# Keeping mLSTM's q and k of a block on the chip, and a shorter ring for the sampled keys while the inputs are projected

## The chip, the cores and the metric

The kernel is one program on one core of a Trainium2 chip. The core has five engines with a queue each: TensorE (PE in the profile; its weight loads are listed apart as PEld), VectorE (DVE), ScalarE (ACT), GpSimd (POOL) and SyncE (SP). Each takes its instructions in the order of the program, and an instruction whose data isn't ready holds up all that stand behind it on that engine. Transfers between DRAM and the on-chip memory (SBUF) are issued here mostly by SP; those that gather rows by an index are issued by POOL. All of them share 16 DMA engines. Matmul results land in PSUM, eight banks of 128 x 512 float32.

The metric is the device time of one execution in microseconds (us), the median of several runs.

## The reference, cut to what matters

One layer of a decoder is computed for 2048 new tokens of one prompt and for 8 sampled sequences of 8 tokens each, which have 8192 earlier tokens in a paged cache.

```python
z = x @ w_in                                    # 1024 -> 3600 columns
fq, fk, fv, f_gate = ...                        # FoX: 8 heads of 64
qk_in, mv, i_gate, f_gate, o_gate = ...         # mLSTM: 4 heads of 128
qk = silu(conv4(qk_in))                         # causal, 4 taps, per channel
mq, mk = qk[..., :512], qk[..., 512:] * 128**-0.5
# FoX: attention with a decay, s += L_q - L_k, softmax, @ v
#   prompt: 2048 x 2048 causal; sampled: 8 x (8192 cached + 8 new)
# mLSTM, chunk by chunk:
Wqk = exp(Dm - m_t) * (q @ k.T)
num = Wqk @ v + (q @ C) * a                     # C: 128 x 128 per head
h   = num / max(|Wqk.sum() + (q @ n) * a|, exp(-m_t))
C   = g * C + (w_key * k).T @ v                 # carried to the next chunk
mix = concat([fox_h, norm(h) * w * o_gate]) @ w_o
x1  = LN(alpha * x + mix)
y   = LN(alpha * x1 + relu(x1 @ w1)**2 @ w2)
```

All is float32. The large products are made of three matmuls with rounded high and low halves (`mm3`), whose halves ScalarE (`split_hi`) and VectorE (`split_lo`) make.

## The kernel before, in words

The program runs in four stages, one after the other.

**Stage A**, the input projection (`block_a`), goes over four blocks of 512 prompt tokens; the first also has the 64 sampled tokens. In a block the columns come in this order: mLSTM's v, mLSTM's q and k (eight groups `j` of 128 channels, each followed by its convolution `conv`), the output gate, FoX's q, k and v. For each piece of 256 columns or tokens, 24 matmuls go into one of four PSUM banks `pm`, and ScalarE or VectorE takes the bank away. In `conv` ScalarE copies the bank into `qi` (two buffers), VectorE multiplies and adds four times into `ac`, ScalarE takes the tanh into `th`, and VectorE makes `(th + 1) * ac`. `ac` and `th` share three buffers. The result is stored to the DRAM array `dqk` (line 468).

**Beside** stage A run two side streams, Python generators that give out a few instructions at each `yield`. `tick(us)`, called after each piece of the projection with the piece's nominal time, takes one step of a stream whenever the summed time passes a pace. The instructions of a step are placed behind the projection's last ones. A scheduler then orders each engine's queue.

- The first stream holds mLSTM (`PACE_M` 2.3): `gate_stream` makes the decay rows of a block, `m_block` goes over its four chunks of 128 tokens, and `m_sample` does the sampled tokens after the first block. A chunk loads its q and k from `dqk` into `qk`, one buffer (`m_load_qk`, line 592). `m_sample` goes over four heads, and each loads its states into `C0`, in the same buffer as `qk` (line 748), and stores them.
- The second is the sampled attention (`sample_attention`). A prologue computes the decays over the cache (in the first stream, ahead of `m_block(0)`). Then come 294 numbered steps (`PACE_A` 7.5). Step `n` gathers piece `n` of the keys (128 x 1024 float32, POOL, `k_gather`, line 1376), turns piece `n-2` in 32 x 32 squares on VectorE (`k_turn`, line 1382, two instructions a piece), and at every fourth step TensorE multiplies four pieces with the queries (`qk_step`, lines 1405 and 1412). The pieces live in `KB`, three pairs of two. Every eighth `qk_step` is followed at once by `softmax` (line 1424), and later steps weigh the values (`v_gather`, `pv_step`, line 1517).

The time of stage A's first block is added to the second stream's account although it has no stream yet, so that at the start of block two some nineteen steps are due at once.

**Stage B** is the prompt's FoX attention. It gives the sampled attention no step (`PACE_B` is infinite). It begins with keys that are loaded, doubled by POOL (`twice`, line 866), transposed by TensorE (line 885) and split. **Stage O** applies `w_o` and the first norm, **stage C** the MLP in four blocks. The sampled attention goes on beside both (`PACE_C` 5).

Of the kernel before, what the change touches and what calls it, by code (L numbers as in the profile page):

```python
# [20 lines left out]
PACE_A = 7.5  # L21
PACE_B = float('inf')
PACE_C = 5
PACE_M = 2.3
# [28 lines left out]
def body(ctx, tc, I, O, stages):  # L53
# [8 lines left out]
    dqk = drm.tile([8, 128, TOT], F32, name="dqk")  # L62
# [34 lines left out]

    acc = [0.0, None, PACE_A]
    macc = [0.0, []]
    last = {}  # L100

    vx = dict(more=None, live=[], next=0, of={})

    def take_back():

        vx["more"] = None
        while 1 in vx["live"] and acc[1] is not None:
            if beside(acc[1]) == 0:
                acc[1] = None
# [7 lines left out]

    def tick(us):

        macc[0] += us  # L120
        while macc[1] and macc[0] > PACE_M:
            macc[0] -= PACE_M
            if beside(macc[1][0]) == 0:
                macc[1].pop(0)
# [3 lines left out]
        while acc[1] is not None and acc[0] > acc[2]:  # L128
            acc[0] -= acc[2]
            if beside(acc[1]) == 0:  # L130
                acc[1] = None
# [272 lines left out]
    def block_a(bi):  # L404
# [31 lines left out]
        macc[1].insert(0, gate_stream(bi))  # L436

        for j in range(8):
# [20 lines left out]
            def conv(src, dst, n):  # L459
                ac = pa.tile([128, 512], F32, name="ac", tag="ac", bufs=3)[:, :n]  # L460
# [4 lines left out]
                th = pa.tile([128, 512], F32, name="th", tag="ac", bufs=3)[:, :n]  # L465
                A.activation(th, ac, AF.Tanh)
                V.scalar_tensor_tensor(th, th, 1.0, ac, op0=OP.add, op1=OP.mult)
                SY.dma_start(dst, th)

            conv(lambda q: qi[:, q:q + 512], dqk[j, :, t0:t0 + 512], 512)  # L470
            if pre:
                conv(lambda q: qs[:, :, q:q + 8], dqk[j, :, S:], 64)
# [32 lines left out]
        for j in range(4):  # L505
            if j % 2 == 0:
                wh, wl = wload([(j * 128, 256)])
                if pre:
                    qr = ps_.tile([32, 8, 8, 8], F32, name="qr", bufs=1)
            cs = slice((j % 2) * 128, (j % 2) * 128 + 128)  # L510
            st = pa.tile([128, 512], F32, name="qst", tag="ac", bufs=3)
            for i in range(2):
# [9 lines left out]
                A.activation(st[:, i * 256:i * 256 + 256], ps[:, w - 256:], AF.Copy, scale=0.125)  # L522
            SY.dma_start(dq[j, :, t0:t0 + 512], st)
            if pre and j % 2 == 1:
                SY.dma_start(dqb[0, :, :, j // 2 * 64:j // 2 * 64 + 64].rearrange("b p c -> p b c"), qr.rearrange("p b i t -> p b (i t)"))
        for i in range(2):
# [10 lines left out]
            natural(sink, (512 + i * 256, 256))  # L537
        for i in range(2):
# [9 lines left out]
    dqkv = dqk.rearrange("j p t -> p j t")  # L548
# [41 lines left out]
    def m_load_qk(c):  # L590
        qk = pm.tile([128, 8, 128], F32, name="qk", bufs=1)
        SY.dma_start(qk, dqkv[:, :, c * 128:c * 128 + 128])
        return qk

# [11 lines left out]
    def m_block(bi):  # L606
# [6 lines left out]
        qk = m_load_qk(bi * 4)  # L613
# [4 lines left out]
        for c in range(bi * 4, bi * 4 + 4):  # L618
            Cs = mst["C"]
            t0 = c * 128  # L620
            yield 1
# [27 lines left out]
            for p in range(2):  # L649
                yield 1  # L650
                if p == 1 and c % 4 < 3:
# [965 lines left out]
```

## Time and profile before

| | |
|---|---|
| median of 3 runs | 3457.11 us (3455.04 to 3475.27) |
| the profiled execution | 3461.98 us, of which 3460.3 us from first to last instruction |
| TensorE busy | 3291.5 us (95%) |
| VectorE, ScalarE, GpSimd busy | 2170.0, 1365.9, 876.3 us |
| granted TensorE clock, mean | 0.975 |
| moved by DMA | 663.16 MB |

Stage A ends about 1000 us after the start, stage B about 1420 us; the rest is O and C. A row of the stretches shows, for a window of time, each engine's busy time with the number of its instructions, the clock that TensorE was granted, and the DMA engines' busy share. A row of the waits says which engine's instruction stood idle, what it waited for, and then the total, the number and the longest of these waits in us. In a timeline, the bracket at the end of a row is the engine's idle time just before it and what ended it.

### The profile page before, as it was taken

The numbers are of one execution on the slowest core, as the hardware profiler recorded it, in microseconds if no ns is written. First come the engines' busy times: TensorE is split into PE (matmuls) and PEld (weight loads), VectorE is DVE, ScalarE is ACT, GpSimd is POOL, SyncE is SP. The second block draws the span as 40 slices with busy tenths as digits, with TensorE's granted clock in tenths as the row PEclk, the third lists the DMA queues.
The fourth block names the chain that finished last, engine by engine and source line by source line (L and its number), as shares of the span: only waits on it lengthen the run. The fifth ranks groups of instructions, "written<-read, shape, count | busy, mean of one in ns | idle before, by whom it ended". The sixth has DMA issues, their size and how long they took to land.

```text
span 3460.3 us, 59595 instructions
## 1 busy us (share of the span) xinstructions
PE 3291.5 (95%) x22428; PEld 2695.6 (78%) x22428; DVE 2170.0 (63%) x5282; ACT 1365.9 (39%) x2818; POOL 876.3 (25%) x962
## 2 busy tenths in 40 slices
PE   8899999898989999999799999999999999999998
PEld 8898888887976767677577777777776777888887
DVE  4948646655658877556566667766666545755455
ACT  3333233332448888622233233332333333443332
POOL 0023122232332222266423333423333110100000
PEclk9899899999999999999899999999999999999999
DMA  5577676776772232377776866868668554442221
GB/s 172 145 211 251 190 210 220 236 240 198 240 221 79 80 82 65 108 260 264 270 241 228 278 234 239 315 208 300 243 209 296 202 179 155 153 137 74 86 86 64
DMA packets 446040, 663.16 MB, mean 192 GB/s; under 512 B 84604, under 2 KB 333760, under 8 KB 444856
## 3 DMA queue, kind: packets, MB, share of 16 engines
q1 hardware_dynamic: 369064, 380.13, 36.3%
q0 software_dynamic: 74304, 270.57, 21.3%
q10 hardware_dynamic: 2384, 8.65, 0.7%
q8 instruction: 177, 2.90, 0.3%
q14 instruction: 111, 0.91, 0.1%
HBM read 598.01 MB, written 61.22 MB: 191 GB/s over the span
## 4 chain that ended last, share of the span: by engine, by line
PE 42%; DMA 4%; issue 2%; DVE 1%; POOL 1%; ACT 0%; SPq 0%; POOLq 0%; ACTq 0%; DVEq 0%
PE py L147 7%; PE py L148 6%; PE py L149 6%; PE ph L147 6%; PE ph L148 6%; PE ph L149 6%; PE sO L1517 2%; DMA wr<-w 2%; PE sQ L1405 1%; DMA kT<-cache_k,idxK 1%; DMA vt<-cache_v,idxV 1%; PE sT L1474 1%; DVE wl L142 0%; DMA y_prompt<-y 0%; POOL kT L1376 0%
## 5 line engine op out<-in xcount | busy, mean ns | idle before, releaser
L1206 DVE TENSOR_TENSOR y<-y,py 128x512 f32<-128x512 f32 (+1 forms) x476 | 320.5, 680 | 267.8 <-PE py L149 263.7
L147 PE MATMUL ph<-x1h,wh 128*128 128x512 f32 (+1 forms) x1280 | 454.3, 355 | 6.4 <-ACT wh L139 5.1
L1382 DVE STREAM_TRANSPOSE kT<-kT 128x512 f32<-128x512 f32 x512 | 330.0, 685 | 199.2 <-DMA kT<-cache_k,idxK 198.9
L149 PE MATMUL ph<-x1h,wl 128*128 128x512 f32 (+1 forms) x1280 | 452.4, 355 | 2.1 <-DVE wl L142 2.0
L148 PE MATMUL ph<-x1l,wh 128*128 128x512 f32 (+1 forms) x1280 | 453.6, 355 | 0.0
L139 ACT ACTIVATE wh<-wr 128x1024 fp32r<-128x1024 f32 x264 | 273.0, 1056 | 439.6 <-PE py L149 232.1
L1376 POOL DMA_INDIRECT kT<-cache_k,idxK x256 | 262.1, 1024 | 715.1 <-PE sQ L1405 645.8
L147 PE MATMUL py<-wh,hh 128*128 128x512 f32 (+1 forms) x1088 | 432.3, 399 | 8.2 <-DVE y L1206 7.7
L148 PE MATMUL py<-wl,hh 128*128 128x512 f32 (+1 forms) x1088 | 427.7, 393 | 0.9 <-DVE wl L142 0.9
L149 PE MATMUL py<-wh,hl 128*128 128x512 f32 (+1 forms) x1088 | 426.6, 393 | 0.0
L142 DVE TENSOR_TENSOR wl<-wr,wh 128x1024 fp32r<-128x1024 f32 x264 | 328.4, 1249 | 90.4 <-PE ph L149 33.0
L147 PE MATMUL pm<-whi,xh 128*128 128x256 f32 (+2 forms) x1088 | 323.9, 298 | 3.5 <-DVE xl L142 2.7
L148 PE MATMUL pm<-wlo,xh 128*128 128x256 f32 (+2 forms) x1088 | 314.8, 289 | 0.0
L149 PE MATMUL pm<-whi,xl 128*128 128x256 f32 (+2 forms) x1088 | 314.1, 289 | 0.0
L147 PEld LDWEIGHTS ph<-x1h,wh 128*128 128x128 f32 x1280 | 241.7, 189 | 46.4 <-ACT wh L139 5.7
L149 PEld LDWEIGHTS ph<-x1h,wl 128*128 128x128 f32 x1280 | 241.2, 189 | 38.5 <-DVE wl L142 4.0
L148 PEld LDWEIGHTS ph<-x1l,wh 128*128 128x128 f32 x1280 | 241.5, 189 | 35.4 <-issue 2.1
L147 PEld LDWEIGHTS py<-wh,hh 128*128 128x128 f32 (+1 forms) x1088 | 201.3, 185 | 64.3 <-DVE y L1206 12.1
L149 PEld LDWEIGHTS py<-wh,hl 128*128 128x128 f32 (+1 forms) x1088 | 201.3, 185 | 50.4 <-issue 3.3
L147 PE MATMUL pm<-xh,whi 128*128 128x256 f32 (+1 forms) x768 | 227.2, 296 | 8.9 <-ACT qi L456 8.9
L148 PEld LDWEIGHTS py<-wl,hh 128*128 128x128 f32 (+1 forms) x1088 | 201.5, 185 | 43.1 <-issue 2.9
L149 PE MATMUL pm<-xh,wlo 128*128 128x256 f32 (+1 forms) x768 | 225.0, 293 | 0.0
(364 smaller groups left out, 6823.5 us busy)
## 6 DMA issues: line engine op xcount, KB each, us to landing
wr<-w SPq DMA_DIRECT2D x256, 512.0 KB
wra<-w_in SPq DMA_DIRECT2D x112, 512.0 KB
xn<-x_prompt SPq DMA_DIRECT2D x32, 512.0 KB
Rb<-dR SPq DMA_DIRECT2D x128, 128.0 KB
dqk<-th SPq DMA_DIRECT2D x32, 256.0 KB
qk<-dqk SPq DMA_DIRECT2D x16, 512.0 KB
qn<-dq SPq DMA_DIRECT2D x128, 64.0 KB
wr<-w_o SPq DMA_DIRECT2D x16, 512.0 KB
```

The costliest lines, as they stand in the source:

```text
L139: last["ACT"] = A.activation(dst, src, AF.Copy, scale=scale)
L142: r = (eng or V).tensor_tensor(dst, src, hi.bitcast(F32), op=OP.subtract)
L147: T.matmul(ps, wh, xh, start=first, stop=False)
L148: T.matmul(ps, wh, xl, start=False, stop=False)
L149: last["PE"] = T.matmul(ps, wl, xh, start=False, stop=stop)
L1206: V.tensor_tensor(y, y, ps, op=OP.add)
L1376: G.indirect_dma_start(out=piece(n), out_offset=None, in_=ck, in_offset=IO(ap=idxK[:, b, j // 2, j % 2:j % 2 + 1], axis=0))
L1382: V.transpose(x, x)
L1405: r = T.matmul(pq[h4 * 32:h4 * 32 + 32, hg].rearrange("p (k f c) -> p k f c", k=2, f=4), z["qb"][:, hd], kv, start=(db == 0), stop=(db == ...
L1474: T.transpose(p[:, f], z["U"][u][:, hg, f].rearrange("p k t -> p (k t)"), ident)
L1517: after_ = T.matmul(po[r:r + 32], z["PT"][:, hg, 2 * f + g, pg].rearrange("p h q -> p (h q)"), vts[f][:, g, hg * 256:(hg + 1) * 256], star ...
```

## The change

q and k of a whole block stay in SBUF: `conv` writes its last product straight into `mst["qk"]`, four chunks of 8 x 128, one buffer for the block; the tanh goes into the space of `qi`, so that `ac` has its two buffers to itself. The stores to `dqk` and the loads of `m_load_qk` are gone, but for the 64 sampled tokens. Before the convolution of the next block begins, what is left of the `m_block` before it is placed.

The sampled attention becomes the second stream from the first block on, prologue included, at pace 5.6, and starts its steps once block one's sampled keys are made. In stage A its ring has two pairs, that is the four pieces of one `qk_step`; two pieces are gathered in each of the first two steps of a group of four, and two are turned in each of the last two. After 19 groups it stops (`yield 3`). Behind stage A a new ring of three pairs is made in a pool of its own, and six pieces are gathered into it at the start of stage B. `softmax` comes one step after the last `qk_step` instead of in the same one, and `softmax_new` two steps after that.

`m_sample` loads the states of a head one head ahead, in the two buffers of tag `vt` that later hold the values. FoX's q is stored in two halves of 256 tokens instead of one of 512.

```diff
-PACE_A = 7.5
+PACE_A = 5.6
-    dqk = drm.tile([8, 128, TOT], F32, name="dqk")
+    dqk = drm.tile([8, 128, NS], F32, name="dqk")
...
+        while mst.get("open"):
+            beside(macc[1][0]) or macc[1].pop(0)
+        mst["qk"] = pm.tile([128, 4, 8, 128], F32, name="qk", bufs=1)
         for j in range(8):
...
-            def conv(src, dst, n):
-                ac = pa.tile([128, 512], F32, name="ac", tag="ac", bufs=3)[:, :n]
+            def conv(src, th, out):
+                n = th.shape[1]
+                ac = pa.tile([128, 512], F32, name="ac", bufs=2)[:, :n]
...
-                th = pa.tile([128, 512], F32, name="th", tag="ac", bufs=3)[:, :n]
                 A.activation(th, ac, AF.Tanh)
-                V.scalar_tensor_tensor(th, th, 1.0, ac, op0=OP.add, op1=OP.mult)
-                SY.dma_start(dst, th)
-            conv(lambda q: qi[:, q:q + 512], dqk[j, :, t0:t0 + 512], 512)
+                V.scalar_tensor_tensor(out, v(th), 1.0, v(ac), op0=OP.add, op1=OP.mult)
+            conv(lambda q: qi[:, q:q + 512], qi[:, 0:512], mst["qk"][:, :, j])
...
-    def m_load_qk(c):
-        qk = pm.tile([128, 8, 128], F32, name="qk", bufs=1)
-        SY.dma_start(qk, dqkv[:, :, c * 128:c * 128 + 128])
-        return qk
...
+        def state(h):
+            c = ps_.tile([128, 8, 128], F32, name="C0", tag="vt", bufs=2)
+            SY.dma_start(c, I["state_C"][0, :, h].rearrange("b d e -> d b e"))
+            return c
...
+        C0s = [state(0), state(1)]
...
         for h in range(4):
-            C0 = pm.tile([128, 8, 129], F32, name="C0", tag="qk", bufs=1)
-            SY.dma_start(C0[:, :, 0:128], I["state_C"][0, :, h].rearrange("b d e -> d b e"))
-            G.tensor_copy(C0[:, :, 128], n0[:, :, h])
-            for _ in range(4):
-                yield 1
+            C0 = C0s[h]
+            yield 1
+            if 1 <= h < 3:
+                C0s.append(state(h + 1))
...
         if bi == 0 and gen:
-            macc[1].append(prologue(gen))
+            acc[0], acc[1] = 0.0, gen
...
+    kx["ring"] = pk_.tile([128, 3, 2, 1024], F32, name="kT", bufs=1)
+    acc[1] = acc[3]
+    if acc[1] is not None:
+        attend()
...
-    KB = ps_.tile([128, 3, 2, 1024], F32, name="kT", tag="kT", bufs=1)
+    kx["ring"] = pa.tile([128, 2, 2, 1024], F32, name="kT", tag="kT", bufs=1)
+    GA = 19
+    NA = 4 * GA
...
-        if 2 <= n < 258:
+        g, r = divmod(n - 2, 4)
+        if 0 <= g < GA and r >= 2:
+            k_turn(4 * g + 2 * r - 4)
+            k_turn(4 * g + 2 * r - 3)
+        if NA + 2 < n < 258:
+            if n == NA + 3:
+                k_turn(NA)
             k_turn(n - 2)
...
-            if g % 8 == 7:
-                softmax(g // 8)
+        b = at(n, 35, 32)
+        if b is not None and b < 8:
+            softmax(b)
...
-        if n < 256:
+        g, r = divmod(n - 2, 4)
+        if 0 <= g < GA and r < 2:
+            k_gather(4 * g + 2 * r)
+            k_gather(4 * g + 2 * r + 1)
+        if NA + 6 <= n < 256:
             k_gather(n)
...
     for n in range(294):
         yield 1
         step(n)
+        if n == NA + 2:
+            yield 3
+            for i in range(6):
+                k_gather(NA + i)
```

94 lines of the change are left out of this document (54 added, 40 removed).

## The prediction, made before the changed kernel ran

> **What bounds the kernel now.** I read the page's first two parts, then the stretches of the stages, then the waits. TensorE is busy nearly all the time, and its clock dips in the first 30% and at a few later places:
>
> ```profile
> PE 3291.5 (95%) x22428; PEld 2695.6 (78%) x22428; DVE 2170.0 (63%) x5282; ACT 1365.9 (39%) x2818; POOL 876.3 (25%) x962
> PEclk9899899999999999999899999999999999999999
> ```
>
> The stretches are stage A, B, and O with C:
>
> ```profile
> 0.00:1000.00 1000.00, 911.90 (x7686) 857.82 (x7686) 621.39 (x1727) 333.27 (x720) 228.82 (x272) 0.95 0.68 210
> 1000.00:1420.00 420.00, 408.92 (x2806) 288.10 (x2804) 334.46 (x1326) 346.67 (x974) 111.56 (x195) 0.98 0.32 88
> 1420.00:3460.00 2040.00, 1970.71 (x11940) 1549.65 (x11939) 1214.15 (x2229) 685.92 (x1125) 535.91 (x495) 0.99 0.60 204
> ```
>
> Stage A takes 29% of the span and has half of TensorE's idle time: 1000 - 911.9 = 88.1 us, against 11.1 in B and 69.3 in O and C. And its clock was 0.95: another 0.05 x 1000 = 50 us in which TensorE counts as busy and does nothing more. So A holds some 138 us that aren't work. What an idle TensorE costs beyond its own time is seen around two stalls (third last column: the granted clock):
>
> ```profile
> 842.70:845.70 3.00, 0.04 (x1) 0.00 (x0) 0.00 (x0) 1.27 (x2) 2.26 (x3) 1.00 0.93 322
> 845.70:859.40 13.70, 4.19 (x49) 4.20 (x50) 5.49 (x18) 0.41 (x1) 0.55 (x1) 0.50 0.53 196
> 187.90:190.40 2.50, 0.61 (x6) 0.62 (x6) 1.22 (x1) 1.42 (x3) 1.06 (x2) 1.00 1.00 281
> 190.40:193.80 3.40, 3.40 (x18) 3.40 (x18) 0.00 (x0) 1.53 (x5) 0.63 (x1) 0.50 0.98 269
> ```
>
> A long stall at 843 us is followed by 13.7 us at half clock, but an idle stretch of 2.5 - 0.61 = 1.9 us at 188 us by 3.4 us at half clock too, in which TensorE is busy throughout. Over A each idle microsecond brings 50 / 88.1 = 0.57 us of lost clock; I count a wait that goes at 1.57 times its length.
>
> The Trainium skill, page "TensorE: Matmul & The Clock Gate", section "HAM oscillation — how this bites in real kernels", gives the rule that gaps over about 3.4 us are what drops the clock. The row of 187.9 differs: 1.9 us idle were enough. By the page only the waits of 3.4 us and longer would carry lost clock; the gain worked out below would be some 5 us smaller.
>
> Which waits are these? TensorE's in stage A, in us, number, longest:
>
> ```profile
> PE px L271 <- DMA xn<-x_prompt: 15.8, 6, 6.7
> PE sQ L1424 <- DVE mxs L1412: 12.5, 1, 12.5
> PE mm L631 <- DMA qk<-dqk: 9.8, 3, 6.5
> PE pm L147 <- ACT qi L456: 9.7, 3, 7.6
> PE mr L325 <- DVE rows L332: 7.8, 2, 5.1
> PE px L481 <- ACT qi L456: 6.8, 1, 6.8
> PE px L271 <- DMA xn<-x_sample: 4.4, 1, 4.4
> PE mm L755 <- DMA C<-state_C: 4.2, 3, 3.1
> PE mm L571 <- POOL hh L566: 4.0, 3, 2.0
> PE mm L631 <- DVE st L498: 3.1, 1, 3.1
> PE pm L147 <- DVE xl L142: 2.7, 2, 1.5
> PE mm L755 <- DVE gm L397: 2.4, 1, 2.4
> ```
>
> **The change part by part.**
>
> *The store of q and k.* The second wait names VectorE's maximum of the scores, but that is not the cause. VectorE's timeline:
>
> ```profile
> 839.96 0.07 DVE L1412 DVE_READ_ACCUMULATOR2_ANT mxs<- 128x1 f32 x1
> 853.82 0.55 DVE L462 TENSOR_SCALAR ac<-qi,cw 128x512 f32<-128x512 f32 x1 [13.78 <-DMA dqk<-th]
> ```
>
> and, earlier,
>
> ```profile
> 88.15 0.55 DVE L462 TENSOR_SCALAR ac<-qi,cw 128x512 f32<-128x512 f32 x1 [8.12 <-DMA dqk<-th]
> ```
>
> After one of four maxima the next convolution stands in VectorE's queue. It needs a buffer `ac`, and that one is still being stored to `dqk`; the three other maxima wait behind it, and TensorE's softmax matmul behind them. At 80 us the same store holds VectorE for 8.1 us while the gate rows (line 332) stand behind it: TensorE's wait of 5.1 us. The change has no such store, and `ac` comes free when VectorE itself has read it. Off: 12.5 + 5.1 = 17.6 us. `softmax` a step later adds nothing here; VectorE's work is the same.
>
> *The load of q and k.* 9.8 us of line 631, all waits for the landing of `qk<-dqk`: off. What is late next is the mask chain on POOL, of which TensorE shows nothing. The bytes, from the DMA view of stage A:
>
> ```profile
> DMA packets 198845, 210.10 MB, mean 210 GB/s; under 512 B 29865, under 2 KB 171388, under 8 KB 198751
> ...
> dqk<-th SPq DMA_DIRECT2D x32, 256.0 KB
> qk<-dqk SPq DMA_DIRECT2D x16, 512.0 KB
> ```
>
> Store and load are 16 MB of the 210; I give their absence no price of its own.
>
> *The even pace.* The sampled attention's matmuls in the two stretches after its start:
>
> ```profile
> 270.00:520.00 250.00, 19.68 (x320) 9.11 (x320) 8.46 (x38) 0.94 0.70 218
> 520.00:760.00 240.00, 9.67 (x160) 4.68 (x160) 4.58 (x20) 0.96 0.74 233
> ```
>
> A group is 32 matmuls: nine groups and a softmax in the first stretch, five in the second. The nine bring 9 x 4 x 2 = 72 turns to VectorE, into the middle of the convolutions, and there lies the 7.6 us wait for `qi`, which is copied only when VectorE has left a buffer. At pace 5.6 three blocks give some 26 steps each, 6.5 groups. I take all of the 7.6 off. For the 6.8 us of line 481 (convolution again, beside the prologue) the bounds are 0 and 6.8; I take the middle, 3.4, because the prologue's index arithmetic stays in one step.
>
> *Sampled states a head ahead*: 4.2 us (`C<-state_C`), off: two are loaded at the start, the others while a head is worked on. The states' stores now hold up the value gathers in the same buffers; the values are used only some 35 steps in.
>
> *At no cost*: the tanh in `qi` keeps that buffer for a tanh and a product more, covered by the other buffer, which the matmuls of a whole `j` fill meanwhile; q in halves gives 16 more stores on SP, where 48 issues go; the leftover of `m_block` before a convolution is empty, for in the changed program's order on TensorE the last chunk of each block stands ahead of the next block's convolution.
>
> Sum of the waits that go: 17.6 + 9.8 + 7.6 + 3.4 + 4.2 = 42.6, with the clock 42.6 x 1.57 = 66.9 us.
>
> *What it adds: the ring of one group.* Where VectorE stood for keys in A, and how long a gather takes:
>
> ```profile
> L1382 DVE STREAM_TRANSPOSE kT<-kT 128x512 f32<-128x512 f32 x154 | 98.9, 682 | 51.9 <-DMA kT<-cache_k,idxK 51.9
> ```
>
> ```profile
> DMA to landing us min/median/max: 4.2/8.4/11.3
> ```
>
> Now no piece of the next group can be gathered before a group's `qk_step`. In the old trace POOL also issues four at a time, behind the same matmul, so much of this wait is there already: 51.9 us, of which TensorE shows 3.1 (the wait for `st`, line 498). In the changed order the eight turns stand closer together behind the four gathers. Behind a waiting turn stand `split_lo` of the weights, the gate sums and mLSTM's products. Bounds: 5 us less (the 3.1 goes), or all that the first rival gives. I take two more stalls of 3.1 us, 2 x 3.1 x 1.57 = 10 us, nearest to what 51.9 us of waits have cost so far.
>
> *Six gathers at the start of B.* POOL's timeline:
>
> ```profile
> 988.25 1.06 POOL L1376 DMA_INDIRECT kT<-cache_k,idxK  x1 [9.97 <-PE sQ L1405]
> ...
> 992.11 0.94 POOL L1376 DMA_INDIRECT kT<-cache_k,idxK  x1 [0.31 <-issue]
> ...
> 1004.03 0.39 POOL L866 COPY dup<-dup 128x256 f32<-128x256 f32 x1 [4.51 <-DMA dup<-k_prompt]
> 1006.63 1.29 POOL L914 TENSOR_TENSOR nd<-nl,dmask 128x128 f32<-128x128 f32 x3 [2.20 <-DMA nl<-dnl]
> 1007.85 0.41 POOL L866 COPY dup<-dup 128x256 f32<-128x256 f32 x1
> ```
>
> A gather follows the one before after (992.11 - 988.25) / 3 = 1.29 us, so six hold POOL 7.7 us. In the changed order they stand behind the third mask `nd` and ahead of the second `dup`, which stage B's second group of keys needs. Bounds: 0, if TensorE has other scores, and 7.7 x 1.57 = 12. I take 8: the start of B has little else to do.
>
> *Stages O and C* have the same groups, gathers and pace as before; `softmax` a step later moves waits of a microsecond. I take 0, give or take 10.
>
> Sum: -66.9 + 10 + 8 = -48.9 us on an execution of 3461.98 us (span 3460.3), which is 4.9 us above the median of the runs: 3457.1 - 48.9 = **3408 us**.
>
> **The rivals.**
>
> *The ring holds VectorE (slower).* In A, at each of the 19 groups, VectorE would wait the median landing, 8.4 us, in place of what it waits now: 160 us against 51.9, 108 more. If two thirds reach TensorE, 72 x 1.57 = 113 us come, and -66.9 + 8 + 113 gives +54: 3511 us. It decides once more than a third of the extra 108 us reach TensorE. For it: VectorE is a strict queue and works 62% of A. Against: only 3.1 of 51.9 us have reached TensorE so far.
>
> *The waits change places.* Only the two that the profile ties to a transfer go (17.6 + 9.8, 43 us with the clock), and the others and the ring give back 23 in all: -20, 3437 us. For it: twelve different waits share A's idle time, and another order of the queues makes others.
>
> *More goes.* With 16 MB and the VectorE blocks away, `x_prompt`, the other half of line 481, `hh`, `st` and `gm` go as well, 15.8 + 3.4 + 4.0 + 3.1 + 2.4 = 28.7, x 1.57 = 45: 3363 us.
>
> *It doesn't do what it says.* If gates or states come late, the rest of `m_block` is placed in one lump with nothing beside it, or the new ring waits for memory of stage A and POOL stands at B's start: the gain is eaten, 3460 us.
>
> **How the numbers follow.** Forecast, 3375 to 3430: 0.50. Waits change places: 0.20. More goes: 0.14. The ring holds VectorE: 0.12. Not as said: 0.04. One per cent, 35 us, is about what a measurement of this kernel can tell from no change. Faster by more than that (under 3422) is the forecast but for 0.07 at its upper end, and the case "more goes": 0.57. Slower (over 3492): 0.12. Within: 0.31. The range from 3350 to 3475 leaves out the slow rival and a little of the fast one.
>
> **What would show it.** After: no wait on `dqk` on VectorE, no `sQ` wait of 12 us in the third block, no wait of line 631's successor for a DMA; A's TensorE busy time near 885 us in 940, clock 0.97; groups of scores 6 or 7 a block; `kT` waits on VectorE near 60 us; a wait for `dup` or `nd` of up to 8 us in B's first 20 us. It is wrong if VectorE's `kT` waits are above 100 us and TensorE's waits name VectorE rows right behind them, or if A's clock doesn't rise.

## The result and the profile after

The changed kernel took **3436.18 us** (median of 7 runs, 3428.73 to 3448.89), the kernel before 3460.2 us in the runs beside it (3455.04 to 3475.27). The ratio is **0.9931**, 95% interval 0.9905 to 0.9956: 24 us faster. The forecast was 3408 us, 49 us faster; the rival *waits change places* had 3437.

The profiled execution took 3431.24 us, its span is 3429.5 us. The page's busy time and clock:

```profile
PE 3277.8 (96%) x22428; PEld 2675.2 (78%) x22428; DVE 2166.7 (63%) x5282; ACT 1367.5 (40%) x2818; POOL 892.0 (26%) x958
...
PEclk9999999999989999999899999999999999999999
```

The stretches: stage A (up to the last matmul of the projection), the 35 us behind it, the rest of B (up to the first matmul of `w_o`), and O with C. The columns are the length, the busy time of PE, PEld, DVE, ACT and POOL with the number of instructions, then the granted clock, the DMA share and GB/s.

```profile
0.00:961.50 961.50, 894.75 (x7675) 842.61 (x7676) 615.64 (x1716) 332.23 (x718) 227.64 (x258) 0.98 0.64 198
961.50:996.50 35.00, 18.30 (x84) 11.89 (x84) 17.04 (x72) 13.05 (x38) 14.23 (x26) 0.71 0.84 249
996.50:1422.00 425.50, 421.70 (x2939) 291.86 (x2937) 334.11 (x1314) 356.54 (x994) 111.44 (x183) 1.00 0.27 76
1422.00:3429.00 2007.00, 1943.04 (x11734) 1528.81 (x11734) 1199.91 (x2181) 665.72 (x1072) 538.69 (x492) 0.99 0.60 207
```

The same first three stretches of the kernel before, cut at its own ends of A and B (B ends at 1452 us there, not at the 1420 us that stand in the text ahead of the prediction):

```profile
0.00:995.60 995.60, 909.93 (x7675) 856.38 (x7676) 619.08 (x1718) 332.65 (x718) 226.18 (x268) 0.95 0.68 209
995.60:1030.60 35.00, 24.93 (x128) 17.16 (x126) 21.93 (x90) 19.08 (x55) 10.57 (x23) 0.76 0.92 278
1030.60:1452.00 421.40, 413.60 (x2895) 291.80 (x2894) 330.56 (x1297) 349.04 (x975) 107.42 (x180) 1.00 0.26 73
```

Stage A is 995.6 - 961.5 = 34.1 us shorter. Its idle time fell from 995.6 - 909.9 = 85.7 to 66.8 us. Of the time in which TensorE was busy at half clock I count one half as lost (from the records of the clock): 32.2 us before, 17.9 after. So 18.9 us are idle time, 14.3 us clock, and the matmuls are the same. Behind it 4.2 us come back: the 35 us at the start of B hold 16.7 us of idle time against 10.1, the rest of B 3.8 against 7.8, and the clock makes up the remainder. O is 1.5 us longer, C 2.3 us shorter. Together these are the 30.8 us between the two profiled executions (spans 3460.3 and 3429.5); the medians lie 24 us apart, so some 7 us of the stages' differences belong to these two executions.

Now TensorE's waits in stage A after the change (total, number, longest):

```profile
PE px L278 <- DMA xn<-x_prompt: 16.9, 6, 5.6
PE sO L1541 <- DMA vt<-cache_v,idxV: 7.7, 6, 2.3
PE mm L587 <- POOL hh L582: 7.2, 3, 2.9
PE pm L154 <- ACT qi L469: 5.8, 2, 3.3
PE pm L154 <- ACT ch_n L506: 5.6, 1, 5.6
PE pm L154 <- DVE xl L149: 4.9, 2, 4.0
PE px L278 <- DMA xn<-x_sample: 4.6, 1, 4.6
PE pm L154 <- DVE st L514: 3.7, 1, 3.7
PE px L497 <- DVE scT L489: 2.4, 1, 2.4
PE mn L674 <- ACT hh L604: 2.2, 2, 1.9
...
PE sQ L1448 <- DVE mxs L1436: 0.7, 1, 0.7
...
PE mr L332 <- DVE gnat L319: 0.4, 1, 0.4
```

The waits that the prediction named did go: softmax 12.5 to 0.7, the gate rows 7.8 to 0.4 (for another tile), `qk` 9.8 to nothing, `qi` of the projection 9.7 to 5.8, that of the state transposes 6.8 to 1.0, the states 4.2 to nothing. That is 12 + 7 + 10 + 4 + 6 + 4 = 43 us, as much as the forecast's sum of 42.6, though its parts were cut otherwise. But idle time fell by 18.9 us only. About 24 us have new names: values 7.7, `ch_n` 5.6, `st` 3.7, `scT` 2.4, and `hh`, `xl`, `hh` of ScalarE and others grown by 1 to 4 us each.

One of the new ones in VectorE's timeline:

```profile
807.62 1.30 DVE L1406 STREAM_TRANSPOSE kT<-kT 128x512 f32<-128x512 f32 x2 [5.83 <-DMA kT<-cache_k,idxK]
...
813.02 0.53 DVE L476 TENSOR_SCALAR ac<-qi,cw 128x512 f32<-128x512 f32 x1
813.47 2.48 DVE L1406 STREAM_TRANSPOSE kT<-kT 128x512 f32<-128x512 f32 x4
815.88 0.70 DVE L478 SCALAR_TENSOR_TENSOR ac<-qi,cw,ac 128x512 f32<-128x512 f32 x1
```

and in ScalarE's:

```profile
819.19 0.63 ACT L479 ACTIVATE qi<-ac 128x512 f32<-128x512 f32 x1 [8.92 <-DVE ac L478]
...
824.03 0.56 ACT L506 COPY ch_n<-px 3x512 f32<-3x512 f32 x1
```

VectorE stands 5.8 us for a piece of the keys, works off what is behind it, and then four turn instructions, 2.5 us, stand between the first and the second product of a convolution. ScalarE stood 8.9 us for that convolution, and its copy `ch_n`, for which TensorE waited 5.6 us, came behind.

### The profile page after: what moved, and what is told of

It reads as the page before. It is cut to its first block, busy times and chain, and to the rows that moved or that the text cites. A ratio compares the mean times of both kernels' runs of the same rounds, so it can differ in the third digit from the quotient of the medians.

```text
span 3429.5 us, 59557 instructions
## 1 busy us (share of the span) xinstructions
PE 3277.8 (96%) x22428; PEld 2675.2 (78%) x22428; DVE 2166.7 (63%) x5282; ACT 1367.5 (40%) x2818; POOL 892.0 (26%) x958
## 4 chain that ended last, share of the span: by engine, by line
PE 43%; DMA 4%; issue 2%; DVE 1%; POOL 0%; ACT 0%; POOLq 0%; ACTq 0%; SPq 0%; DVEq 0%
PE py L154 7%; PE py L155 7%; PE py L156 7%; PE ph L154 6%; PE ph L155 6%; PE ph L156 6%; PE sO L1541 2%; PE sQ L1429 2%; DMA kT<-cache_k,idxK 1%; DMA wr<-w 1%; DMA vt<-cache_v,idxV 1%; PE sT L1498 1%; DVE wl L149 0%; DMA y_prompt<-y 0%; PE px L1168 0%
## 5 line engine op out<-in xcount | busy, mean ns | idle before, releaser
L1517 POOL DMA_INDIRECT vt<-cache_v,idxV x158 | 162.6, 1029 | 257.1 <-PE sO L1541 187.2
```

What stands on the lines that cost most here:

```text
L1517: G.indirect_dma_start(out=vt.rearrange("p f c -> p (f c)"), out_offset=None, in_=cv, in_offset=IO(ap=idxV[:, b, (kt % 4) * 4 + kt // 4, f ...
```

## The experiments

The runs fell on several chips, on which the kernel before took 3460 to 3486 us; each ratio is against the kernel before on the same chip. P stands for the runs of the changed kernel itself (before 3460), Q (3482 to 3486), R (3485), S (3486) and T (3464) for the others; the kernel before was profiled on P alone. A stage's time comes from one execution, and executions of one kernel side by side differ by up to 20 us (the changed kernel: 3428.73 to 3448.89), so a few us between two rows mean nothing, least of all between chips. An amount in us beside a ratio is worked out from the ratio. The table has TensorE's idle time in stage A and the clock lost there, worked out as above.

| kernel | ratio, 95% interval | chip | A, us | idle | clock lost |
|---|---|---|---|---|---|
| before | 1 | P | 995.6 | 85.7 | 32.2 |
| changed | 0.9931, 0.9905 to 0.9956 | P | 961.5 | 66.8 | 17.9 |
| e1_dram_trip | 0.9920, 0.9902 to 0.9938 | Q | 977.2 | 72.7 | 21.7 |
| e2_burst | 0.9916, 0.9898 to 0.9935 | Q | 969.2 | 68.5 | 21.0 |
| e3_late_gathers | 0.9932, 0.9911 to 0.9953 | Q | 975.0 | 68.5 | 27.2 |
| b2_even_pace | 0.9937, 0.9918 to 0.9957 | Q | 966.9 | 70.5 | 17.9 |
| e7_burst_and_trip | 0.9926, 0.9905 to 0.9946 | R | 972.6 | 70.5 | 22.3 |
| b3_softmax_later | 0.9994, 0.9980 to 1.0008 | R | 997.2 | 83.6 | 31.6 |
| b4_no_burst | 1.0070, 1.0046 to 1.0095 | R | 942.8 | 70.4 | 23.2 |
| e6_gathers_late | 0.9915, 0.9894 to 0.9935 | R | 975.5 | 68.9 | 27.7 |
| b5_prologue | 0.9974, 0.9963 to 0.9985 | S | 1001.5 | 92.6 | 28.7 |
| b6_prologue_even | 0.9993, 0.9978 to 1.0007 | S | 1000.0 | 85.3 | 31.8 |
| e4_states_in_head | 0.9920, 0.9903 to 0.9937 | S | 975.7 | 70.3 | 26.8 |
| e5_values_first | 0.9912, 0.9892 to 0.9931 | S | 972.4 | 71.1 | 22.0 |
| b7_free_ring | 0.9950, 0.9932 to 0.9968 | T | 977.8 | 74.5 | 25.8 |
| b10_free_ring_even | 0.9868, 0.9850 to 0.9886 | T | 956.1 | 60.0 | 21.2 |
| e8_ring_only | 1.0010, 0.9994 to 1.0025 | T | 1001.5 | 95.3 | 30.1 |
| e10_both_gathers | 0.9895, 0.9878 to 0.9912 | T | 973.2 | 71.5 | 24.6 |
| b13_ring_added | 0.9995, 0.9982 to 1.0007 | Q | 979.0 | 79.1 | 22.5 |
| b11_free_ring_softmax | 0.9939, 0.9921 to 0.9958 | Q | 990.2 | 80.9 | 28.3 |

### One part undone, one part alone

**The DRAM trip put back** into the changed kernel:

```diff
+            thp = pa.tile([128, 512], F32, name="thp", tag="ac", bufs=3)
+            conv(lambda q: qi[:, q:q + 512], thp, thp)
+            SY.dma_start(dqk[j, :, t0:t0 + 512], thp)
...
+        qk = m_load_qk(bi * 4)
```

> The changed kernel, but q and k of the prompt go through DRAM again: conv stores each product to dqk from a buffer shared with ac (three), and a chunk loads its q and k. Pace, ring and states as changed. The changed kernel as a whole stands 24 us under the kernel before (ratio 0.993). Theory 'own price' (each wait that the change took off is worth its length and some clock, wherever it stands): the trip costs the 17.6 + 9.8 us of waits of the old trace, with the measured clock loss (32 us lost in 86 us idle, 1.38) 38 us: 14 us slower than the kernel before, ratio 1.004. Theory 'places change' (a wait taken off lets another come in, so that single parts are worth less): under half of that, about 15 us, ratio 0.9975, and the old waits for dqk come back while others shrink.

0.992: nothing is lost. VectorE still stood 23.9 us for the stores, but of TensorE's waits only 0.9 us are for `qk`, and none is the old one for the softmax. It isn't the trip as such that cost. Neither theory had this number. (It isn't quite the old trip: the sampled product has its own buffers, FoX's q no longer shares the ring of three, and the tile to be stored is taken from the ring ahead of `ac`.)

**The even pace alone**, in the kernel before:

```diff
-PACE_A = 7.5
+PACE_A = 5.6
...
-            acc[1] = gen
+            acc[0], acc[1] = 0.0, gen
```

> The kernel before with one thing of the change: pace 5.6 and an account that starts at zero when the sampled attention gets its turn, so that no burst of steps stands at the start of block two. Own price: the 7.6 us wait for qi and nothing else, with the clock 10 us: ratio 0.997. Places change: the store and load of q and k keep their stalls, at other places; ratio between 0.998 and 1.004. A third possibility: the pace itself does most of the change's work, ratio 0.994.

0.9937: this edit alone gives as much as the whole change, and not by the wait for `qi` alone. The old trip and its ring are still there, but TensorE's wait for the softmax, 12.5 us, is gone, that for the load of q and k is 2.8 in place of 9.8 and that for the gate rows 4.3 in place of 7.8; VectorE's waits of a convolution for stores fell from 27.0 to 15.6 us. So one and the same wait can go by more than one part of the change. (One group of keys moved out of A: 18 in place of 19; O is some 8 us longer than in the profile before.)

**The burst put back** into the changed kernel:

```diff
-PACE_A = 5.6
+PACE_A = 7.5
...
+        if not kx["new"]:
+            acc[0] += 145.0
```

> The changed kernel with the old pace: 7.5, and nineteen steps due at once when block one's sampled keys are made. Own price: 10 us lost against the changed kernel, ratio 0.996. Places change: the values are then weighed at a wider pace, so the 7.7 us of waits of sO for its gathers in stage A go while the burst costs about the same; ratio 0.993.

0.9916: nothing is lost, and the waits for values fell from 7.7 to 3.4 us. So the pace gives 22 us alone and is not missed where the rest of the change is there.

**The six gathers later**, first attempt:

```diff
+            if n == 12 and acc[3] is not None:
+                acc[1] = acc[3]
+                attend()
```

> The changed kernel, but the six gathers into the new ring are issued at unit 12 of stage B in place of its start. If they are what delays the first query loads and the second doubled keys, stage B's first 35 us lose their extra 7 us of idle and the whole is 7 to 9 us faster: ratio 0.9905. If the start of B is slow for another reason (its own loads), no change: 0.993.

The scheduler put the gathers where they were: the order on every queue is that of the changed kernel, but for one pair of neighbours on VectorE ahead of the steps. It is that kernel once more, on another chip: 0.9932 beside 0.9931.

**Burst and trip together:**

> The changed kernel with two parts undone at once: q and k of a block go through DRAM again, and the sampled attention runs at pace 7.5 with nineteen steps due at once at the end of block one. Its shorter ring, its softmax one step later and its states a head ahead stay. Each part undone alone left the ratio at 0.992. Theory 1 (burst and trip cost only together, since a burst of gathers holds the stores that VectorE waits for): the gain is gone, ratio 0.999 to 1.002, and a wait of 10 us or more on a store of dqk reaches TensorE. Rival (what the kernel before lost lies in its softmax at once, or in its states; either is gone here): ratio 0.992 to 0.994. The third (any order of the queues but the old one is as good): also 0.992 to 0.995, with other waits than the old ones.

0.9926. Theory 1, that only the two together cost, falls. (Its edits are those of e1_dram_trip and e2_burst.)

**Softmax a step later alone**, in the kernel before:

```diff
-            if g % 8 == 7:
-                softmax(g // 8)
+        b = at(n, 35, 32)
+        if b is not None and b < 8:
+            softmax(b)
```

> The kernel before with one edit: softmax one step after the last group of scores, softmax_new two steps after that, as in the changed kernel. If the 12.5 us wait of softmax behind a convolution is a loss of its own, it goes: -12.5 us and 5 us of clock, ratio 0.995. If the convolution's wait for the store holds something else in its place (scores and turns stand in the same queue): ratio 0.999 to 1.001.

0.9994, nothing, as the prediction had it for this edit: VectorE's wait for the store stays (15.7 us at the longest).

**The burst taken away, pace 7.5 kept:**

```diff
-            acc[1] = gen
+            acc[0], acc[1] = 0.0, gen
```

> The kernel before with one edit: the sampled attention's account starts at zero, so that no steps are due at once at the start of block two; pace 7.5 stays, and the nineteen steps are done later, in stages O and C. If the burst is what costs: ratio 0.993, stage A's idle time near 70 us. If the steps only move their waits to the other stages: stage A is 20 to 30 us shorter, O and C longer by as much, ratio 0.998 to 1.001.

1.007, slower, which neither theory had. Stage A does six groups of keys and a softmax fewer (14 sets of these matmuls in place of 21) and weighs fewer values, and stage C does them: C took 1862.0 us against 1775.4 in b3_softmax_later on the same chip, 87 us more, where A has 54 us less. The same work is dearer in C than in A. So taking the burst away pays only where A keeps its share of the groups, or all but one.

**The prologue in the second stream**, with the burst and with the even pace:

```diff
-            macc[1].append(prologue(gen))
+            acc[0], acc[1] = 0.0, gen
...
-            while macc[1] and "pro" not in mst:
-                tick(PACE_M)
-            acc[1] = gen
```

> The kernel before with one part of the change: the prologue of the sampled attention runs in the second stream from block one on, beside the projection, and no longer in the first stream ahead of mLSTM; the nineteen steps still come at once at the end of block one, pace 7.5. In the runs so far block one (the first quarter of the projection's matmuls) took 239 to 242 us with the old prologue, and 229 to 234 us in every kernel that has the new one, with or without the DRAM trip. Theory A (the prologue's place is a part of the gain by itself): block one is 8 to 12 us shorter, ratio 0.996 to 0.998. Rival (what block one gains comes back in block two, where mLSTM's own work then stands): ratio 0.999 to 1.001.

> The kernel before with the prologue in the second stream and the even pace of 5.6 from a zero account; the DRAM trip of q and k, the ring of three pairs, softmax at once and the states in their own head all stay. The even pace alone gave 0.9937. Theory A: the two parts add up in stage A, and stage B doesn't pay for a new ring, ratio 0.989 to 0.991, better than the changed kernel. Rival (whatever wait goes, another takes its place, and some 25 us is all that another order yields): ratio 0.992 to 0.995.

0.9974 and 0.9993. The first lies in theory A's range, but the first quarter of A's projection did not get shorter (242 us in both, from the records of its matmuls), so theory A's reason falls, and where the 9 us come from isn't shown. (The premise was too narrow: the old prologue also went with 236 us in b2_even_pace and 237 in b4_no_burst.) And with the prologue moved, the even pace lost the gain that it has alone: VectorE's waits for the stores rose from 15.6 to 38.3 us. An edit that only moves work can take back some 19 us here.

**The states in their own head:**

```diff
-            C0 = C0s[h]
-            yield 1
-            if 1 <= h < 3:
-                C0s.append(state(h + 1))
+            C0 = state(h)
+            for _ in range(4):
+                yield 1
```

> The changed kernel with one part undone: the states of a sampled head are loaded in their own head, four steps ahead of their use, as in the kernel before, still in the buffers of the values. If the wait for the states (4.2 us in the kernel before) is a loss of its own: some 6 us slower than the changed kernel, ratio 0.994 to 0.996. If the four steps cover the load as they do in most heads: 0.992 to 0.994.

0.992, no loss: the head start of the states saves nothing that can be measured.

### The gathers' order

**Values first**: the block with `v_gather` stands ahead of the key gathers in a step. And the **six gathers really late**, by an order on GpSimd's own queue:

```diff
-                G.tensor_tensor(nd, nl[:, qt * 128:n], dmask, op=OP.add)
+                last["POOL"] = G.tensor_tensor(nd, nl[:, qt * 128:n], dmask, op=OP.add)
```

> The changed kernel with the gathers of the values ahead of those of the keys in a step. In the changed kernel TensorE waited 7.7 us in stage A for the values (6 times), which it hardly did before, since now two key gathers stand ahead of a value gather on GpSimd. If these waits are a loss of their own: they go, ratio 0.990 to 0.992. If the keys then come later by as much and VectorE stands for them: ratio 0.993 to 0.995.

> The changed kernel with the six gathers at the start of stage B put behind the mask of its thirteenth unit, some 60 us into the stage, by an order on GpSimd's queue. The run with late gathers before this one turned out to have the order of the changed kernel on every queue: it was that kernel once more (ratio 0.9932). If the six gathers hold up the queries by filling the DMA engines: the first 35 us of stage B lose 7 of their 15 us of idle time, ratio 0.990 to 0.991. If the queries come late for another reason (the stores on SyncE ahead of them): idle time stays at 14 to 16 us and the ratio at 0.993.

0.9912 and 0.9915, against 0.9931 and 0.9932; each interval overlaps theirs. In e5_values_first TensorE still waits 6.3 us for values, so its mechanism isn't shown. That of e6_gathers_late is, for the start of the stage. The first 35 us of stage B, with the gathers there (e3_late_gathers) and without:

```profile
975.00:1010.00 35.00, 19.71 (x90) 12.70 (x88) 17.70 (x72) 13.15 (x39) 14.11 (x26) 0.71 0.86 249
```

```profile
975.50:1010.50 35.00, 25.44 (x138) 17.73 (x138) 24.29 (x100) 19.07 (x55) 10.39 (x24) 0.80 0.79 214
```

Idle time is 35 - 19.7 = 15.3 us with them, 9.6 us without. Most of it comes back further on: over the whole of stage B e6_gathers_late is 1.9 us shorter (458.3 against 460.2), e10_both_gathers below 7.4 us (452.8). In the changed kernel's timelines it is the queries, not the keys, that are late:

```profile
971.24 1.06 POOL L1400 DMA_INDIRECT kT<-cache_k,idxK  x1 [0.16 <-issue]
```

```profile
976.24 1.12 PE L933 MATMUL pS<-ks,qh 128*128 128x384 f32 x2 [5.91 <-ACT qh L146]
```

Both edits together:

> The changed kernel with both small edits that came out best by themselves: the six gathers some 60 us into stage B (0.9915) and the gathers of the values ahead of those of the keys (0.9912). If they add to the 0.9932 of the changed kernel: 0.989 to 0.990. If they are the scatter of one order against another: 0.991 to 0.993.

0.9895, by the ratio 13 us under the changed kernel's 0.9932; its interval ends at 0.9912, where that of e3_late_gathers begins (0.9911), and that of the changed kernel's own runs begins at 0.9905. The intervals touch, so a gain of the two together is likely and not shown. The waits for values are 7.3 us here, so it would not come from there.

### What the store holds, and what the ring takes back

**The ring of the convolution freed**, trip, burst and all else as before:

```diff
...
-                th = pa.tile([128, 512], F32, name="th", tag="ac", bufs=3)[:, :n]
                 A.activation(th, ac, AF.Tanh)
-                V.scalar_tensor_tensor(th, th, 1.0, ac, op0=OP.add, op1=OP.mult)
-                SY.dma_start(dst, th)
+                V.scalar_tensor_tensor(ac, th, 1.0, ac, op0=OP.add, op1=OP.mult)
+                SY.dma_start(dst, ac)
...
+            conv(lambda q: qi[:, q:q + 512], pa.tile([128, 512], F32, name="ac", tag="ac", bufs=3), qi[:, 0:512], dqk[j, :, t0:t0 + 512])
```

> The kernel before, still storing q and k to DRAM and loading them again, still with the burst, but with the tanh in the space of qi and the product made in place, so that a convolution needs one ring buffer in place of two (and the sampled one has small buffers of its own): no convolution has to wait for the store just made. Theory S (the store's hold on the ring is the price that the change takes off; the trip itself is free): VectorE's waits of a convolution for dqk, 27 us, fall under 5; TensorE's waits for the softmax in block three (12.5 us) and for the gate rows in block one (5.1 us) go; ratio 0.992 to 0.995. Rival W (a freed wait is taken up by another within the same block): stage A's idle time stays at 80 us or more, ratio 0.998 to 1.000.

0.995, 17 us. Its waits in stage A, of TensorE and of VectorE:

```profile
PE sT L1453 <- ACT Sn L1443: 14.8, 1, 14.8
...
DVE ac L461 <- DMA dqk<-ac: 13.6, 3, 6.7
...
DVE acs L461 <- DMA dqk<-acs: 9.6, 3, 7.5
...
PE mn L664 <- DVE Cs L667: 8.2, 1, 8.2
...
PE mr L325 <- DVE rows L332: 1.7, 1, 1.7
...
PE mm L630 <- DMA qk<-dqk: 1.5, 1, 1.5
```

VectorE still waits 13.6 + 9.6 = 23 us for stores, not under 5 as I had expected, but no longer where TensorE needs it: the softmax's 12.5 us are gone and the gate rows' are 1.7. The first quarter of the projection, where the gate rows stood, goes with the convolution's code across all runs: it took 236 to 242 us in the seven kernels with the old convolution, e8_ring_only among them, and 228 to 234 us in the thirteen with another one. The wait for the load, 9.8 before, is 1.5, though every load is still there. And close to where the softmax stood there is a new wait of 14.8 us. What released it, in ScalarE's timeline:

```profile
842.01 1.06 ACT L139 ACTIVATE whi<-wra 128x1024 fp32r<-128x1024 f32 x1 [13.32 <-DMA wra<-w_in]
...
843.50 0.71 ACT L1441 ACTIVATE S<-S,m 128x512 f32<-128x512 f32 x1
```

The exponentials stand behind a split of weights, for whose load ScalarE stood 13.3 us. Some 39 us of the old waits are gone (12.5, 6.1 of the gate rows, 8.3 of `qk`, 5.3 and 6.6 of `qi`); idle time is 11.2 us less than in the profile before (74.5 against 85.7, on two chips).

The old stall and the new one have something in common. In the kernel before, the store behind the wait of 13.8 us, and in this one, the load behind that of 13.3 us:

```profile
839.11 0.94 POOL L1376 DMA_INDIRECT kT<-cache_k,idxK  x1 [21.63 <-PE sQ L1405]
...
843.13 0.46 SPq L468 DMA_DIRECT2D dqk<-th  x1
```

```profile
818.32 1.91 POOL L1375 DMA_INDIRECT kT<-cache_k,idxK  x1 [21.80 <-PE sQ L1404]
...
827.43 3.08 SPq L229 DMA_DIRECT2D wra<-w_in  x1
```

Each time GpSimd is issuing six gathers of 512 KB, four of keys and two of values (839.1 to 846.3 us, 818.3 to 829.2 us). The store was issued 5.6 us after its product was made, and let VectorE go 10.7 us after that, at 853.8; the weights were split 14.6 us after the issue of their load, at 842.0. So in both kernels a transfer issued beside the gathers comes late, and the order of the queues decides which engine stands for it. That is read from the two timelines; that the gathers are the cause isn't shown, for no run moves them alone away from there.

**The same with the even pace:**

> The same ring for the convolution in the kernel with the even pace of 5.6 and the zero account (which had 0.9937 by itself). Theory S and an even pace add: 0.988 to 0.990. If both take off the same waits: 0.992 to 0.994. By rival W: anything between 0.993 and 1.000, as the prologue moved beside the even pace lost the whole gain.

**0.9868**, 46 us (42 us by the medians, 3422.18 against 3464.16): the two add, and this beats both kernels without q and k in SBUF, without the short ring and without the states ahead. Idle time in A is 60.0 us. (As in b2_even_pace, A has done 18 groups of keys in place of 19.)

**The freed ring with softmax later:**

> The kernel with the convolution's ring free alone (ratio 0.995), with softmax one step later as well. With the ring free, the old softmax wait of 12.5 us went, but one of 14.8 us came right behind it: softmax_new waits for ScalarE's exponentials, which stand behind a split of weights that waited 13.3 us for its load. If a later softmax takes that off: 14.8 us and some 5 us of clock, ratio 0.989 to 0.991. If the split of the weights holds ScalarE in any case and another matmul waits for it: 0.994 to 0.996.

0.9939, against 0.9950 without: within what the two intervals leave, nothing. The wait of 14.8 us is gone from its list, and others stand in it: 9.6 us for the states, 7.9 us for `ch_n`.

**Five parts undone, the ring kept** (the edits of e7_burst_and_trip and e4_states_in_head, the old `conv`, softmax at once):

> The changed kernel with five parts undone: q and k go through DRAM with the old three buffers of the convolution, the burst at the end of block one, softmax in the step of the last scores, and the states loaded in their own head. What stays is the ring of two pairs with its rhythm (four gathers in two steps, two turns in two steps), the new ring at the start of stage B, the prologue in the second stream and the halves of FoX's q. By theory S the waits for dqk are back: ratio 0.999 to 1.002. If the ring's rhythm carries the gain that all kernels with it had: 0.992 to 0.994.

1.001. So the ring's rhythm isn't what carries the gain. The old waits are back:

```profile
PE mm L645 <- DMA qk<-dqk: 10.6, 1, 10.6
PE sQ L1451 <- DVE mxs L1439: 8.7, 1, 8.7
```

**The ring alone added** to b10_free_ring_even:

```diff
-        if 2 <= n < 258:
-            k_turn(n - 2)
+        if 0 <= g < GA and r >= 2:
+            k_turn(4 * g + 2 * r - 4)
+            k_turn(4 * g + 2 * r - 3)
...
+        if n == NA + 2:
+            yield 3
+            for i in range(6):
+                k_gather(NA + i)
```

> The best kernel so far (the kernel before with the convolution's ring free and the even pace, ratio 0.9868), with one part of the change added: the ring of two pairs in stage A with its rhythm (four gathers in two steps, two turns in two steps, nineteen groups and then a stop) and six gathers at the start of stage B. Memory and all the rest stay. The changed kernel has these two savings, the load of q and k and the states off too, and still only 0.9931. Theory R (the ring takes back what the other parts gain): VectorE's waits for keys rise from 47 us to over 65, stage B's first 35 us have 15 us of idle time in place of 8, ratio 0.992 to 0.995. Rival: the ring costs what it does in B alone (5 us) or nothing, ratio 0.987 to 0.989, and the loss lies in the other parts (prologue, states, softmax, halves of q).

0.9995: the ring takes back all 44 us. Its waits in stage A:

```profile
DVE kT L1396 <- DMA kT<-cache_k,idxK: 51.1, 26, 6.0
...
DVE ac L467 <- DMA dqk<-ac: 13.7, 1, 13.7
...
PE mm L636 <- DMA qk<-dqk: 9.2, 3, 6.9
...
PE pm L153 <- ACT ch_n L495: 7.9, 1, 7.9
```

VectorE waits for keys 51.1 us, hardly more than the 47.3 us of b10_free_ring_even; that part of theory R is wrong, and the loss is larger than it had. Beside b2_even_pace on the same chip A is 12 us longer, and B 14 us, of which 10 lie in the gap up to its first scores (18.3 us in place of 8.3). Of the gap, the nineteenth group, left over at A's end and placed alone, is a part that the changed kernel doesn't have. Which of the ring's pieces costs how much in A wasn't separated, and not without the trip either.

## Why the prediction was right or wrong

*The store of q and k* and *The load of q and k*: the cause was right (a convolution that holds VectorE's queue until a store is done), and the waits went. The price failed. Forecast: (17.6 + 9.8) x 1.57 = 43 us. With the hold on the ring taken off by itself, both waits went (12.5 us to nothing, 9.8 to 1.5) and 17 us were gained. The load needs no price of its own: its wait nearly goes with the ring freed (1.5 us) and with the even pace alone (2.8 us), though every load is still there; why isn't shown. And a stall of 12.5 us, when it goes, leaves what stood in its shade: 14.8 us for exponentials. **This is the step that failed**: each wait was counted at its full length, as if nothing else were late at the same place. In the changed kernel 43 us of named waits went, and idle time fell by 18.9 us. The prediction asked what is late next only for the load, and named the mask chain on GpSimd. It also gave each wait to one part: the softmax's 12.5 us, put to the store alone, go with the even pace too, while the stores stay.

*The even pace*: forecast 11 x 1.57 = 17 us; measured 22 us alone, and 28 us beside the freed ring (0.9950 to 0.9868; 25 us by the medians). The size is near, the cause is right in part: the waits for `qi` fell (9.7 to 3.5 us, 6.8 to 5.0), but the larger part is the softmax's and the load's, which the forecast had given to the store. And it is not the burst as such: the changed kernel loses nothing with the burst put back.

*Sampled states a head ahead*: forecast 6.6 us, measured none.

*Softmax a step later adds nothing*: right, alone and beside the freed ring.

*What it adds*: forecast 10 + 8. If the changed kernel has the 46 us that b10_free_ring_even saves, its 24 us mean that it gives back some 20 us. But that is a subtraction between two kernels whose parts don't add, not a measurement, and the ring added to b10_free_ring_even took 44 us. VectorE's waits for keys rose from 51.9 to

```profile
DVE kT L1406 <- DMA kT<-cache_k,idxK: 73.2, 30, 6.7
```

and not to the 160 us of *the ring holds VectorE*; no wait of TensorE's names them directly, and in that of 5.6 us for `ch_n` a late piece and four turns have their share. *Six gathers at the start of B*: B is 4.2 us longer by the two profiles, and in e6_gathers_late the first 35 us lose 5.7 us of idle time and the whole stage 1.9 us, beside a forecast of 8. But no wait for `dup` or `nd` shows there. The queries came late. A second candidate for what was given back is the prologue, whose move the forecast gave no cost: moved beside the even pace, it took 19 us, and no run undoes it in the changed kernel.

*The clock*: 0.57 us per idle microsecond was taken from the mean clock of stage A, which counts half-clock stretches in which TensorE was idle too. Counted only where it was busy, it is 32.2 / 85.7 = 0.38. Between the two kernels it was 14.3 / 18.9 = 0.76, from one execution each, and two executions of the changed kernel's order alone (the changed kernel and e3_late_gathers) differ by 9.3 us of lost clock. So the runs neither confirm nor refute 0.57. The error isn't there: with 0.38 the waits of 42.6 us would still have come to 59 us, and stage A is 34 us shorter.

*Stages O and C* at nothing: right, within 2.3 us.

In all: stage A was to lose 67 us and get 10 back, and lost 34 (894.75 us busy in 961.5, not 885 in 940); B was to get 8, and got 4. The case *waits change places* had 3437 us, within one microsecond of the median, and it was given 0.20. The figure is luck in part: it stood on 3457.1 us before, where the runs beside it have 3460.2, so it had 20 us off and 24 were measured; and its account, that only the two waits tied to a transfer go, doesn't fit, since the others that were named went or shrank too, and new ones came. What holds is what spoke for it: twelve different waits share A's idle time, and another order of the queues makes others.

Open is why the parts don't add. The changed kernel misses neither the trip, the burst, nor both; the kernel before gains from the freed ring and from the even pace; the short ring costs 44 us beside the trip, and e1_dram_trip, which has both, is as fast as the changed kernel. The runs show the sizes, not a rule for them.

## What to carry to other kernels

A sum of waits in one crowded stage is no forecast of what an edit takes off: here it was too high for the store and the load (43 us against 17) and too low for the pace (17 against 22). For each large wait, find what else was late at that moment, above all on the engine just behind and among the transfers issued beside it. Before spending memory to take a transfer away, free the buffer that the transfer holds: here two small edits (a product made in place, an even pace) gave 1.3%, and the large one, which paid for its memory with a shorter ring, 0.7%; that ring, added to the two small edits, took their gain back. And an order of work is a part of a kernel's time: where many streams share in-order queues, try each part alone and each part undone.

## What the runs showed of the hardware

Two executions of the changed kernel's order (the changed kernel and e3_late_gathers) took 961.5 and 975.0 us for stage A; idle time is 66.8 and 68.5 us, the clock lost 17.9 and 27.2 us. So 9 of the 13.5 us are the granted clock alone. The kernel before took 3460 us beside the first and 3486 beside the second, so the chips differ; how much of the 9 us is the chip and how much the single execution isn't shown.

The idle time ahead alone sets neither whether the clock drops nor for how long. Two gaps of nearly the same length, in b10_free_ring_even (4.9 us, of which the first row shows 3.9) and b13_ring_added (4.6 us, of which it shows 4.2):

```profile
879.40:883.30 3.90, 0.00 (x0) 0.00 (x0) 0.35 (x1) 3.90 (x12) 1.44 (x6) 1.00 0.21 58
883.30:893.50 10.20, 9.27 (x49) 6.84 (x50) 6.25 (x10) 1.27 (x5) 4.79 (x5) 0.50 0.81 235
```

```profile
815.10:819.30 4.20, 0.01 (x1) 0.00 (x0) 3.36 (x8) 0.69 (x2) 0.00 (x0) 1.00 1.02 410
819.30:822.70 3.40, 3.03 (x14) 3.03 (x15) 3.00 (x13) 2.53 (x4) 0.00 (x0) 0.50 0.62 243
```

After the first the clock is at one half for 10.2 us, after the second for 3.4 us, both about a multiple of 3.4. And a gap of 3.3 us in the changed kernel, after which the clock stays at 1.00:

```profile
562.00:565.60 3.60, 0.29 (x3) 0.12 (x2) 0.40 (x1) 1.48 (x4) 0.20 (x1) 1.00 0.53 176
565.60:574.00 8.40, 6.33 (x52) 6.12 (x52) 5.41 (x11) 8.40 (x26) 0.00 (x0) 1.00 0.22 63
```

The Trainium skill, page "TensorE: Matmul & The Clock Gate", section "HAM oscillation — how this bites in real kernels", lets gaps over about 3.4 us drop the clock: these three gaps agree with that, the prediction's row of 187.9 us, where 1.9 us were enough, doesn't. The rule doesn't tell how long the clock stays low.
